# Macaron block on one core: mix norm of rows 6 and 7 traced ahead of the last product's row norms, weight splits ordered behind the last silu or copy

## The chip, the cores and the metric

One core of a Trainium2 chip runs the whole program in one launch. The metric is device microseconds of that core: the median of three runs, and beside it one execution taken by the hardware profiler, to which all rows of the trace belong.

## What is computed

The reference is one layer of an encoder trunk on x of 1024 tokens by 1024 features, all in float32:

```
x = x + 0.5 * RMSNorm_post(SwiGLU_1(RMSNorm_pre(x)))      # d_ff 2816
h = RMSNorm_pre(x); q/k/v = h @ w_qkv
heads = concat(8 grouped-query heads, 8 dilated-window heads)
x = x + RMSNorm_post(heads @ w_out)
x = x + 0.5 * RMSNorm_post(SwiGLU_2(RMSNorm_pre(x)))
SwiGLU(x) = (silu(x @ w_gate) * (x @ w_up)) @ w_down
```

## The kernel before, in words

**Precision.** Every product of matrices is made from a high and a low part of each operand, in three passes (high·high, high·low, low·high). So each loaded weight is split: ScalarE (ACT) copies it to the high part, and GpSimd (POOL) or VectorE (DVE) subtracts that from the weight for the low part. `split` (lines 117 to 119) does this; ACT's half shows as line L118, the other as L119.

**Gate and up.** `Ffn` works through columns i of the hidden width, 1 to 21 (column 0 is done plainly before). A column takes seven products P1 ... P7 instead of eight, from sums of blocks of the operands; `ORDER` gives their order as P1, P6, P2, P7, P5, P4, P3 (the last column has an order of its own). Each product is twelve matmuls at L294 into one of the PSUM banks a, b, c, d. P1 and P2 both accumulate in bank a: after P1, ACT copies the bank to the tile u2 (L416), and only then may P2's matmuls write there, with one product (P6, in bank b) between them. The others are added into u2, u3 and c21 by DVE (L418, L421, L424, L430, L433). `glu` then takes the silu on ACT (L449) and multiplies it with the up half on DVE (L450). In every odd column `keep` writes combinations of the finished hidden tiles to DRAM.

**The weights ahead.** The ring `wgu` has five buffers. `feed` runs before each product and calls `prepare` until five products' weights are made, so ahead of product n the splits of product n + 4 are traced. `prepare` issues the loads of the next column's raw weights on SyncE's queue (SP), the block sums on POOL (L215, L216 before P6, with the sums queued behind P1's low part; L225, L227 after P2, the last of which makes P7's operand), and `split_w`. In trace order a split comes after the silu or copy of the product before, but the framework's scheduler orders each engine's instructions itself: an instruction that it takes to be ready sooner is put first, and the engine then works through its queue in that order. `tc.issue_after(ins)` is the means of holding it: what is traced in its block on the engine of `ins` stands behind `ins` in that queue. It adds no instruction and no semaphore.

**Down and the first tail.** The down product also takes seven products per block, in two groups of inner blocks. `run` goes through all items; a table of jobs gives what is traced after which item, counted from the first item of down product 1 of the second group. For the first FFN the jobs do the work of rows 4 to 7 beside the last two down products: `stat1` (row sums of squares), `post1` (post norm, residual, store of the row tile to `x1d`; L547, L548, L549), `mix1` (the mixing stage's norm: a square with row sum on ACT, L100; a root on ACT, L80; five small operations on DVE; a scale in place on ACT, L647) and `turn1` (eight transposes into PSUM, L107, then high and low part to `actT`, L108 and L109). The last down product, k = 6, finishes rows 0 to 3: for each, `row1` calls `post_late` (half-row square on ACT, L568) and, every second row, `post_scale` (L544, L545) with the store to `x1d`.

**Into the projection.** After `run`, `first(j, T)` is one block of the q/k/v projection: 24 matmuls at L608 for row tile T with weight set j, then an ACT copy (L618), a DVE low part (L619) and two stores. `split_q(1)` splits the second weight set on ACT and DVE (L595, L596). `first(1, 4)` is the first block that needs all of it. The squares of `mix1` write their unused output to slots of `actT`: rows 6, 0, 2 to slot 2, rows 7, 1, 3 to slot 3; `post_late` writes into slot 3 as well:

```
def mix1(Ts):
    r = rms_pair([y[:, T, :] for T in Ts], [junk(T % 2 + 2) for T in Ts])
    for n, T in enumerate(Ts):
        ACT.activation(y[:, T, :], y[:, T, :], AF.Copy, scale=r[n])

def post_late(T):
    ACT.activation(actT[:, HI, 4:8, 3], y[:, T, 512:1024].rearrange("p (k f) -> p k f", k=4), AF.Square,
                   accum_out=SS[T // 2][:, 1, T % 2:T % 2 + 1])
```

So in trace order the square of row 7 came after the four of `post_late`, on one engine.

Of the kernel before, what the change touches and what calls it, by code (L numbers as in the profile page):

```python
# [13 lines left out]
AF = mybir.ActivationFunctionType  # L14
# [22 lines left out]
def tile_macaron_block(ctx, tc, x, f1_pre, f1_post, f1_g, f1_u, f1_d, mix_pre, mix_post, w_qkv,  # L37
                       qg, kg, w_out, f2_pre, f2_post, f2_g, f2_u, f2_d, rope_a, rope_b, mask, out):
    nc = tc.nc
    PE, ACT, DVE, POOL, SP = nc.tensor, nc.scalar, nc.vector, nc.gpsimd, nc.sync  # L40
# [80 lines left out]
    class Ffn:  # L121
# [18 lines left out]
        def __init__(self, wg, wu, wd, tag, far):  # L140
            self.wg, self.wu, self.wd, self.tag, self.far = wg[0], wu[0], wd[0], tag, far
            self.near = "left" if far == "right" else "right"
            self.W, self.RAW, self.H, self.P, self.B, self.Q = {}, {}, {}, {}, {}, {}
            self.A, self.S = {}, {}
            self.items = [("G", i, p) for i in range(1, NF) for p in (self.ORDER if i < NF - 1 else self.LAST)]
            downs = [("D", k, j) for n, g in enumerate(self.GROUPS) for k in self.DOWN[n] for j in g]
            self.items += downs
            self.tiles = []
            for it in self.items:
                self.tiles += [it] if it[0] == "G" else [it + (z,) for z in range(2)]  # L150
            self.wanted = [d[1:] for d in downs]
            self.hd = {}
            for key in self.wanted:
                self.hd[key] = dram.tile([128, 512], F32, name=f"hd{tag}" + "_".join(str(z) for z in key))
            self.made = self.used = 0
            self.dw = {}
            self.late, self.late2 = [], []

        def open_raw(self):
# [48 lines left out]
        def prepare(self, i, prod):  # L208
            a1, b1, a2, b2 = [self.RAW[i, d][:, :, :, 64 * b:64 * b + 64] for d in range(2) for b in range(2)]
            sub, add, tt = OP.subtract, OP.add, POOL.tensor_tensor  # L210
            if i + 1 < NF and prod in ("P1", "P4"):
                self.load_gu(i + 1, ("P1", "P4").index(prod))
            if prod == "P6":
                with tc.issue_after(self.order):
                    tt(b1, b1, b2, op=add)  # L215
                tt(a1, b1, a1, op=sub)  # L216
            if prod == "P7" and i == NF - 1:
                self.S["x"] = self.raw.tile([128, 2, 4, 128], F32, name="rawgu")[:, :, :, 0:64]
                tt(self.S["x"], b2, a1, op=sub)
            src = {"P1": a1, "P6": a1, "P7": self.S.get("x", a1), "P5": b1, "P2": a2, "P4": b2, "P3": a2}[prod]  # L220
            ins = self.split_w((i, prod), src, DVE if (i, prod) == (1, "P6") or prod in ("P5", "P3") else POOL)
            if prod == "P1":
                self.order = ins
            if prod == "P2":
                tt(a2, a2, a1, op=sub)  # L225
                if i < NF - 1:
                    tt(a1, b2, a1, op=sub)  # L227
# [174 lines left out]
        def gate_up(self, i, prod, ps, y, psd):  # L402
            def U(name):
                return self.u.tile([128, 4, 128], F32, name=name, bufs=2 if name == "U2" else 1)

            tt, add, s = DVE.tensor_tensor, OP.add, self.S
            n = (self.ORDER if i < NF - 1 else self.LAST).index(prod)
            if i == 1 and 0 < n < 5:
                self.turn_combo(("T2", "T3", "T1", "T4")[n - 1], y, psd)
            p = self.bank(i, ps, self.BANK[prod])  # L410
            first = prod in ("P1", "P6", "P7", "P5")
            name = {"P1": "B11", "P6": "T2", "P7": "T3", "P5": "T1", "P2": "B21", "P4": "T4", "P3": "B22"}[prod]
            self.product(p, self.W[i, prod], name, first)
            if prod == "P1":
                s["u2"], s["c21"] = U("U2"), U("C21")
                ACT.activation(s["u2"], p, AF.Copy)  # L416
            elif prod == "P6":
                tt(s["u2"], s["u2"], p, op=add)  # L418
            elif prod == "P7":
                s["u3"] = U("U3")  # L420
                tt(s["u3"], s["u2"], p, op=add)  # L421
            elif prod == "P5":
                s["h1"] = self.new_h(i, 1)
                tt(s["u3"], s["u3"], p, op=add)  # L424
                self.glu(s["h1"][64:128], s["u3"], s["c21"])
            elif prod == "P2":
                s["h0"] = self.new_h(i, 0)
                self.glu(s["h0"][0:64], p, s["h0"])
            elif prod == "P4":
                tt(s["c21"], s["u2"], p, op=add)  # L430
                self.glu(s["h0"][64:128], s["c21"], s["h0"])
            elif prod == "P3":
                tt(s["u2"], s["u2"], p, op=add)  # L433
                self.glu(s["h1"][0:64], s["u2"], s["c21"])
            if i == NF - 1 and n == 3:
                self.close_tx(3)
                self.raw.release()
                self.load_left(self.AHEAD)
                self.open_blocks(("b11", "b12"), self.far)
                self.open_blocks(("b22", "b21"), self.near)  # L440
                for j in self.GROUPS[0]:
                    self.load_block(j, "b21")
            if n == 6 and i % 2 == 1:
                self.keep(i // 2)
            if n == 6 and i == NF - 1:
                self.U = [U(name).rearrange("p t f -> p (t f)") for name in ("U2", "U2", "C21", "U3")]

        def glu(self, dst, c, s):
            ACT.activation(s[64:128], c[0:64], AF.Silu)  # L449
            DVE.tensor_tensor(dst, s[64:128], c[64:128], op=OP.mult)  # L450

        def run(self, ps, y, psd, jobs, row):
# [83 lines left out]
    def junk(T):  # L536
        return actT[:, HI, :, T]
# [106 lines left out]
# [4 lines that stand above are left out]
# [9 lines left out]
    def turn1(T):  # L657
        to_actT(T, y[:, T, :], psd)

    def row1(i):  # L660
        post_late(i)
        if i % 2 == 1:
# [5 lines left out]
    f1.run((psg0, psg1), y, psd,  # L668
           {0: [begin1, lambda: stat1((4, 5)), lambda: post1(4)], 1: [lambda: post1(5)], 3: [lambda: mix1((4, 5))],
            5: [early1], 6: [first_q], 7: [lambda: stat1((6, 7)), lambda: post1(6)], 8: [lambda: post1(7)],  # L670
            9: [lambda: turn1(4), lambda: turn1(5)]}, row1)
    psg1.release()
    psg0.release()
    wq1 = open_pool("wq1", side="right")
# [3 lines left out]
    def first(j, T):  # L678
        store_v(j, T, qkv_mm(j, T, psq), wq1)

    mix1((6, 7))
    mix1((0, 1))
    turn1(6)
    first(0, 4)
    turn1(7)
    first(0, 5)
    mix1((2, 3))
    split_q(1, wq1, raw1, "wq1")
    first(0, 6)
# [39 lines left out]
    for nm, g, sc in (("k", kg, None), ("q", qg, 0.125)):  # L729
# [5 lines left out]
        for hf in range(2):  # L735
            for rc in range(2):
                o = 32 * rc + 16 * hf
                s = 32 * rc + 16 * (1 - hf)
# [127 lines left out]
    for j in range(2, 9):  # L866
# [10 lines left out]
        for T in range(NT):  # L877
            p = qkv_mm(j, T, psq)
# [184 lines left out]
    for t in range(NT + 2):  # L1063
        if t < NT:
# [3 lines left out]
            p = pso.tile([128, 1024], F32, name="pz")  # L1068
# [136 lines left out]
```

## Time and profile before

| | us |
|---|---|
| median of 3 runs (lowest, highest) | 2038.99 (2038.28, 2039.86) |
| the profiled execution's own time | 2038.71 |
| its span, first to last instruction | 2036.9 |
| PE (TensorE) busy | 1976.9 |
| ACT busy | 1030.5 |
| DVE busy | 1351.0 |
| POOL busy | 840.7 |

A row of the timeline gives start and length in us, engine, line, operation, output<-inputs by the program's names, shapes and count; in brackets the time that the engine stood idle before it and what ended that. PEld is the load of a matmul's stationary operand, which overlaps the matmul before. A row of the windows gives each engine's busy time in a stretch, then TensorE's granted clock (1.00 is 2.4 GHz, 0.50 is 1.2 GHz) and the share of the DMA engines.

### The profile page before, as it was taken

Reading aid. Unit: us, or ns where it says so; the run is one execution under the profiler, and the core shown is the slowest. Engines: PE = TensorE matmul, PEld = TensorE weight load, DVE = VectorE, ACT = ScalarE, POOL = GpSimd, SP = SyncE. Lnnn points to the kernel's source line nnn. Section 1 sums busy time; section 2 is a strip of 40 time slices with the busy share of each in tenths; the row PEclk is TensorE's granted clock in tenths of the full one; section 3 lists DMA queues with packets and bytes.
Section 4 is the critical chain, followed back from the end, with each engine's and each line's share of the span. In section 5 each row is a group of like instructions: output and inputs, shape, how many; then the busy total and the mean of one; then the engine's idle time right before and its main releaser. Section 6 shows DMA issues by size and latency. Waiting matters only on the chain.

```text
span 2036.9 us, 30471 instructions
## 1 busy us (share of the span) xinstructions
PE 1976.9 (97%) x10704; PEld 1675.1 (82%) x10704; DVE 1351.0 (66%) x2435; ACT 1030.5 (51%) x1977; POOL 840.7 (41%) x768
## 2 busy tenths in 40 slices
PE   7999999999999899999999999999999999999996
PEld 6777777778878699998999998887777777788785
DVE  7645554557878838756989888356545455577787
ACT  5433333334445734547999999234333333344444
POOL 4566656560000002124777887315565666600000
PEclk9999999999999899999999999999999999999998
DMA  5232332428534542232050743322223232375343
GB/s 150 74 102 95 113 103 79 130 82 274 182 109 144 183 131 78 78 93 59 1 140 13 205 133 93 104 78 73 94 88 121 86 104 93 109 268 176 120 130 138
DMA packets 212441, 235.62 MB, mean 116 GB/s; under 512 B 22209, under 2 KB 148161, under 8 KB 212161
## 3 DMA queue, kind: packets, MB, share of 16 engines
q1 hardware_dynamic: 212288, 233.69, 36.7%
q8 instruction: 84, 1.38, 0.3%
q14 instruction: 69, 0.56, 0.1%
HBM read 166.01 MB, written 67.63 MB: 115 GB/s over the span
## 4 chain that ended last, share of the span: by engine, by line
PE 70%; POOL 11%; ACT 6%; DVE 5%; issue 4%; DMA 3%; SPq 0%; DVEq 0%; ACTq 0%; POOLq 0%
PE pq L608 10%; PE pd L368 8%; PE pa L294 8%; PE pc L294 6%; PE pd L294 5%; PE pt L935 5%; POOL wgu L119 5%; PE pz L1073 4%; PE pb L294 3%; PE pa L368 3%; ACT wgu L118 3%; PE po L959 3%; PE pb L368 3%; PE pc L368 3%; PE sp L845 3%
## 5 line engine op out<-in xcount | busy, mean ns | idle before, releaser
L119 POOL TENSOR_TENSOR wgu<-rawgu,wgu 128x512 fp32r<-128x512 f32 x216 | 312.9, 1457 | 359.5 <-ACT wgu L118 333.4
L118 ACT ACTIVATE wgu<-rawgu 128x512 fp32r<-128x512 f32 x302 | 181.7, 628 | 377.6 <-POOL rawgu L227 189.6
L294 PE MATMUL pa<-actT,wgu 128*128 128x512 f32 (+1 forms) x1080 | 268.2, 395 | 7.9 <-ACT U L416 7.9
L294 PEld LDWEIGHTS pa<-actT,wgu 128*128 128x128 f32 x1080 | 197.1, 189 | 63.5 <-ACT U L416 20.1
L368 PE MATMUL pd<-wgu 128*128 128x512 f32 x948 | 236.3, 393 | 7.5 <-DVE wgu L119 6.9
L368 PEld LDWEIGHTS pd<-wgu 128*128 128x128 f32 x948 | 178.3, 189 | 49.2 <-DVE wgu L119 10.6
L608 PE MATMUL pq<-wq,actT 128*128 128x256 f32 x1728 | 217.4, 283 | 0.6 <-DVE actT L109 0.6
L608 PEld LDWEIGHTS pq<-wq,actT 128*128 128x128 f32 x1728 | 208.4, 189 | 1.4 <-DVE actT L109 0.9
L118 ACT ACTIVATE wgu<-b 128x512 fp32r<-128x512 f32 x154 | 97.2, 631 | 218.9 <-PE pd L368 209.6
L73 POOL TENSOR_SCALAR gpost<-gpost 128x1024 f32<-128x1024 f32 x2 | 2.6, 1294 | 387.5 <-DVE wgu L119 194.5
L838 POOL TENSOR_SCALAR P<-P,il 128x1024 f32<-128x1024 f32 (+1 forms) x128 | 130.5, 1020 | 66.7 <-DVE il L837 62.7
L119 DVE TENSOR_TENSOR wgu<-b,wgu 128x512 fp32r<-128x512 f32 x154 | 106.1, 689 | 76.5 <-ACT wgu L118 76.4
L450 DVE TENSOR_TENSOR h<-h,C 64x512 f32<-64x512 f32 x42 | 49.6, 1182 | 160.8 <-ACT h L449 160.8
L939 DVE TENSOR_TENSOR PT<-pt,PT 128x512 fp32r<-128x512 f32 (+1 forms) x256 | 146.0, 611 | 2.0 <-ACT PT L938 2.0
L294 PE MATMUL pc<-actT,wgu 128*128 128x512 f32 x552 | 136.5, 395 | 0.0
L294 PE MATMUL pd<-actT,wgu 128*128 128x512 f32 x552 | 136.0, 395 | 0.0
L938 ACT ACTIVATE PT<-pt 128x512 fp32r<-128x512 f32 (+1 forms) x256 | 125.2, 544 | 12.3 <-PE pt L935 8.8
L935 PE MATMUL pt<-identr,P 128*128 128x128 f32 x896 | 124.9, 274 | 2.0 <-ACT vst L773 1.0
L294 PEld LDWEIGHTS pd<-actT,wgu 128*128 128x128 f32 x552 | 103.4, 187 | 25.3
L294 PEld LDWEIGHTS pc<-actT,wgu 128*128 128x128 f32 x552 | 103.4, 188 | 25.3 <-DVE actT L109 0.4
L294 PE MATMUL pb<-tx,wgu 128*128 128x512 f32 x504 | 122.9, 392 | 0.0
L294 PE MATMUL pc<-tx,wgu 128*128 128x512 f32 x504 | 122.4, 392 | 0.0
(204 smaller groups left out, 3978.6 us busy)
## 6 DMA issues: line engine op xcount, KB each, us to landing
hd<-h SPq DMA_DIRECT2D x154, 256.0 KB, 2.8
h<-hd SPq DMA_DIRECT2D x154, 256.0 KB, 2.9
rawgu<-in_ffn_w_gate_dram SPq DMA_DIRECT2D x88, 256.0 KB, 3.0
rawgu<-in_ffn_w_up_dram SPq DMA_DIRECT2D x88, 256.0 KB, 3.5
b<-in_ffn_w_down_dram SPq DMA_DIRECT2D x88, 256.0 KB, 3.6
bkT<-kd SPq DMA_DIRECT2D x32, 320.0 KB, 7.6
rawq<-in_w_qkv_dram SPq DMA_DIRECT2D x16, 512.0 KB, 4.9
bV<-vd SPq DMA_DIRECT2D x8, 640.0 KB, 3.9
```

The source lines that it names most:

```text
L118: ACT.activation(hi, raw, AF.Copy)
L119: return eng.tensor_tensor(lo, raw, f32(hi), op=OP.subtract).ins
L294: PE.matmul(p[:, c0:c1, :], w[:, a, k, :], self.rhs(name, b, k)[:, c0:c1, :], start=(first and n == 0), stop=(n == 11), skip_group_check=True)
L368: PE.matmul(p, A[:, a, 128 * i:128 * i + 128], B[:, b, :], start=(first and start and j == js[0] and n == 0), stop=(end and j == js[-1] an ...
L608: PE.matmul(p, actT[:, a, k, T, :], WQ[j][:, b, k, :], start=(n == 0), stop=(n == 23))
L838: POOL.tensor_scalar(P[:, 0:w], P[:, 0:w], il, 1.0, op0=OP.mult, op1=OP.mult)
L845: PE.matmul(sp[:, 512 * half:512 * half + 512], col(qT[:, h, :], T), kT[:, a, 512 * half:512 * half + 512], start=(a == 0), stop=(a == 1))
L935: PE.transpose(out=p[:, j, :], in_=col(P, b0 + j), identity=ident)
L938: ACT.activation(hv, p[:, 0:n, :], AF.Copy)
L939: DVE.tensor_tensor(lv, p[:, 0:n, :], f32(hv), op=OP.subtract)
L959: PE.matmul(o, V[:, k, :], pt[:, a, k, :], start=(n == 0), stop=(n == 15))
L1073: PE.matmul(p[:, 512 * dh:512 * dh + 512], actT[:, a, c, T, :], WO[c][:, b, 512 * dh:512 * dh + 512], start=(n == 0), stop=(n == 23))
```

## The change

Two things. First, each ACT instruction that is P1's copy or a silu of `glu` is remembered as `self.mark`, and the ACT half of every gate/up split that `prepare` makes is queued behind the mark that was last set when it is traced. The splits of the down products, and those traced before the first copy, get no such edge. Second, `mix1((6, 7))` moves from behind `run` into the job after item 9, where it stands ahead of `turn1(4)`, `turn1(5)` and of the last down product with its `row1` calls; and `mix1((0, 1))` moves behind `turn1(6)`, `first(0, 4)`, `turn1(7)`, `first(0, 5)`.

```diff
-            self.dw = {}
+            self.dw, self.mark = {}, None
...
-            ins = self.split_w((i, prod), src, DVE if (i, prod) == (1, "P6") or prod in ("P5", "P3") else POOL)
+            with ExitStack() as behind:
+                if self.mark is not None:
+                    behind.enter_context(tc.issue_after(self.mark))
+                ins = self.split_w((i, prod), src, DVE if (i, prod) == (1, "P6") or prod in ("P5", "P3") else POOL)
...
             if prod == "P1":
                 s["u2"], s["c21"] = U("U2"), U("C21")
-                ACT.activation(s["u2"], p, AF.Copy)
+                self.mark = ACT.activation(s["u2"], p, AF.Copy).ins
...
         def glu(self, dst, c, s):
-            ACT.activation(s[64:128], c[0:64], AF.Silu)
+            self.mark = ACT.activation(s[64:128], c[0:64], AF.Silu).ins
...
-            9: [lambda: turn1(4), lambda: turn1(5)]}, row1)
+            9: [lambda: mix1((6, 7)), lambda: turn1(4), lambda: turn1(5)]}, row1)
...
-    mix1((6, 7))
-    mix1((0, 1))
     turn1(6)
     first(0, 4)
     turn1(7)
     first(0, 5)
+    mix1((0, 1))
     mix1((2, 3))
```

## Rows read from the trace of the kernel before

**Rows 1.** The page: busy time of each engine, and the clock in 40 slices.
```profile
PE 1976.9 (97%) x10704; PEld 1675.1 (82%) x10704; DVE 1351.0 (66%) x2435; ACT 1030.5 (51%) x1977; POOL 840.7 (41%) x768
...
PEclk9999999999999899999999999999999999999998
```

**Rows 2.** Waits of PE: who waited for whom, us in total, times, longest.
```profile
PE pa L294 <- ACT U L416: 7.9, 18, 2.2
...
PE pd L107 <- ACT y L647: 4.1, 1, 4.1
```

**Rows 3.** Timeline of PE: starts of P1 in six columns, and one P2.
```profile
77.88 2.96 PE L294 MATMUL pa<-actT,wgu 128*128 128x512 f32 x12
...
97.33 2.96 PE L294 MATMUL pa<-actT,wgu 128*128 128x512 f32 x12
...
142.36 3.07 PE L294 MATMUL pa<-actT,wgu 128*128 128x512 f32 x12 [0.24 <-ACT U L416]
...
452.23 2.96 PE L294 MATMUL pa<-actT,wgu 128*128 128x512 f32 x12
...
1408.70 2.96 PE L294 MATMUL pa<-actT,wgu 128*128 128x512 f32 x12
...
1428.10 2.96 PE L294 MATMUL pa<-actT,wgu 128*128 128x512 f32 x12
...
1782.75 2.96 PE L294 MATMUL pa<-actT,wgu 128*128 128x512 f32 x12
```

**Rows 4.** Timeline of ACT in one column whose P1 starts at 156.35.
```profile
157.20 0.63 ACT L118 ACTIVATE wgu<-rawgu 128x512 fp32r<-128x512 f32 x1 [4.67 <-POOL rawgu L227]
157.86 0.63 ACT L449 ACTIVATE h<-C 64x512 f32<-64x512 f32 x1
...
160.57 0.63 ACT L449 ACTIVATE C<-U 64x512 f32<-64x512 f32 x1 [1.42 <-DVE U L433]
161.23 0.60 ACT L416 ACTIVATE U<-pa 128x512 f32<-128x512 f32 x1
```

**Rows 5.** Timeline of DVE in the same column.
```profile
153.75 0.69 DVE L430 TENSOR_TENSOR C<-U,pc 128x512 f32<-128x512 f32 x1 [0.48 <-PE pc L294]
158.52 1.24 DVE L450 TENSOR_TENSOR h<-h,C 64x512 f32<-64x512 f32 x1 [4.08 <-ACT h L449]
```

**Rows 6.** Timeline of POOL and PE: P7's low part made, P7's matmuls.
```profile
157.91 1.29 POOL L119 TENSOR_TENSOR wgu<-rawgu,wgu 128x512 fp32r<-128x512 f32 x1 [0.74 <-ACT wgu L118]
...
164.78 2.92 PE L294 MATMUL pc<-tx,wgu 128*128 128x512 f32 x12
```

**Rows 7.** Windows behind the last down product: engines' busy time, clock, DMA.
```profile
700.50:704.60 4.10, 0.03 (x1) 0.00 (x0) 3.89 (x20) 4.10 (x10) 0.00 (x0) 0.85 0.85 294
704.60:708.20 3.60, 3.60 (x16) 3.28 (x16) 0.55 (x1) 3.60 (x5) 0.00 (x0) 0.50 0.93 286
708.20:713.00 4.80, 4.21 (x19) 3.91 (x19) 4.80 (x9) 4.80 (x12) 0.00 (x0) 0.50 0.68 258
```

**Rows 8.** Timeline of PE in the same stretch.
```profile
694.71 5.81 PE L608 MATMUL pq<-wq,actT 128*128 128x256 f32 x48
...
717.71 3.08 PE L608 MATMUL pq<-wq,actT 128*128 128x256 f32 x24
...
721.41 3.08 PE L608 MATMUL pq<-wq,actT 128*128 128x256 f32 x24
...
728.82 16.38 PE L608 MATMUL pq<-wq,actT 128*128 128x256 f32 x137
```

**Rows 9.** Timeline of ACT in the same stretch.
```profile
694.27 0.63 ACT L568 ACTIVATE actT<-y 128x512 fp32r<-128x512 f32 x1 [4.86 <-DVE y L386]
...
698.79 1.05 ACT L100 ACTIVATE actT<-y 128x1024 fp32r<-128x1024 f32 x1
...
703.40 4.27 ACT L647 ACTIVATE y<-y,rs_y 128x1024 f32<-128x1024 f32 x4
```

**Rows 10.** Stores of row tiles to x1d: from issue to landing, 8 of them.
```profile
DMA to landing us min/median/max: 2.6/3.0/5.8
```

## The prediction

> **What bounds the kernel now.** I read the page first: PE is busy for 97% of the span and its clock is full in all slices but one inside the span and the last [rows 1]. A change that touches only ACT's queue can therefore pay only where PE stands still or runs at half clock. So the next view is PE's waits, and two of them name work that this change moves [rows 2]: matmuls into bank a that waited for P1's copy (7.9 us, 18 times), and the transposes of row 6, which waited once, 4.1 us, for the scale of `mix1`. The reader is to see that the first is spread over the columns and the second is one hole.
>
> **The columns, where the time is.** Idle time understates the first wait, since a late matmul also spoils the overlap with its weight load; the starts of P1 tell it whole. The shortest column of FFN 1 runs from 77.88 to 97.33, 19.45 us; that of FFN 2 from 1408.70 to 1428.10, 19.40 us. From 77.88 to 452.23 there are 19 columns in 374.35 us, and 19 x 19.45 = 369.55: 4.80 us lost. From 1408.70 to 1782.75 there are 19 in 374.05 us, and 19 x 19.40 = 368.60: 5.45 us lost [rows 3]. Together 10.25 us. Of the 7.9 us of idle in the waits, the two longest stand in column 1 of each FFN (2.2 us, the row's longest, and a shorter one of about the same kind), before any mark exists for the splits concerned, and stay.
>
> **Why it is lost.** ACT's queue in one column shows it [rows 4]. c21 was ready at 153.75 + 0.69 = 154.44 [rows 5], yet P4's silu began at 157.86, because P7's split for the next column stood before it and had waited 4.67 us for POOL's L227. DVE, which also works in order, then stood 4.08 us in L450 for that silu [rows 5]; behind L450 is the addition that P3's silu needs, so that silu came at 160.57 and P1's copy at 161.23. P1's matmuls start at 156.35 and a product takes 19.45 / 7 = 2.8 us, so the bank can be copied from about 159.3: the copy is some 1.9 us late and ends only when PE wants bank a, at about 161.9 (P2 of the column before shows 0.24 us of plain idle [rows 3]).
>
> **Part one, the mark.** It adds no instruction, no DMA and no semaphore. P7's split, traced after P4's silu, must now stand behind it. The silu goes at 154.5, L450 at 155.1, the addition as soon as P3 ends at about 156.4, P3's silu near 157.9 (after P7's split, which still comes when L227 ends), the split of P5 after it, and P1's copy at about 159.3, with nothing in front. It ends 2 us before PE needs the bank. I take the whole 10.25 us. From below the bound is the idle that is seen as such: 7.9 less the two waits in column 1, if the second is put at the row's longest too, 3.5 us. What is late next: the splits, which now stand behind silus. P7's low part ends at 157.91 + 1.29 = 159.20 and its matmuls start at 164.78 [rows 6], 5.6 us of cover; a silu is 0.63 us [rows 4], so a split pushed behind one or two stays covered.
>
> The rule that speaks against this part is the strict first-in, first-out queue that the Trainium skill, "TensorE: Matmul & The Clock Gate", section "Architectural detail: the array is 16× 32×32, not 1× 128×128", gives for ScalarE and VectorE: a queued split now inherits each delay of its silu. The 4.67 us of [rows 4] agrees that a queue is held by its head; by that rule alone each split pays for its silu as each silu paid for the split, and it decides the fourth rival's sign, not this sum.
>
> **Part two, the mix norm.** The hole: PE does two blocks from 694.71 (5.81 us), stands until 704.60 waiting for row 6, and runs at half clock from there to 713.00 [rows 7, 8]. The excess over a full-rate run: from 694.71 to 728.82 are seven blocks and six turns of a row. Later, block plus turn take 721.41 - 717.71 = 3.70 us, a block alone 5.81 / 2 = 2.9. So 6 x 3.70 + 2.9 = 25.1 us against 34.1: 9.0 us, the most that this part can give [rows 8].
>
> Why row 6 is late: row 7's square writes the same slot as `post_late`, and in trace order came last, so it stood behind the four half-row squares that begin at 694.27, and went at 698.79; the root and the scales of both rows wait for it, and the scales came at 703.40 [rows 9]. Traced first, it can go in the 4.86 us that ACT stands idle before 694.27, row 7's tile being done in the main by then. It issues no DMA and no POOL work, so nothing moves on SP or POOL; it passes the transposes of rows 4 and 5 with their copies, the last product with its row norms, and on SP the loads of the second weight set, none of which needs it. Its five small DVE operations lie in the same 4.86 us, which DVE's first evacuation ends; without that cover they would delay the row norms. So the transposes of rows 6 and 7 will be ready within the 5.81 us of the two blocks and PE goes straight on.
>
> What is late next is the second weight set, which `first(1, 4)` needs and which ACT splits between its other work. In the hole ACT is busy without a pause: 4.10 of 4.10, 3.60 of 3.60, 4.80 of 4.80 us [rows 7]. It becomes the bound. What leaves it is a square of 1.05 and two scales of 4.27 / 4 = 1.07: 3.2 us. With ACT no longer short, the weight halves, ready early, also go ahead of the squares of rows 2 and 3, two more of 1.05, so `first(1, 4)` moves from 717.71 to about 712.4, 5.3 us earlier. Bounds: 9.0 us above; below, a loss of 2 us: the scale is in place, so row 7's waits until its store to `x1d` has landed, 2.6 to 5.8 us after issue [rows 10], and it could hold the row norms behind it by some two scales. I take 5.3, nearer to the ACT rows than to the full hole.
>
> The clock fell in this stretch after PE had stood idle, and 7.8 us of PE's busy time ran at 1.2 GHz [rows 7]; at 2.4 GHz that is half, so 3.9 us of the 9.0 is the clock's. The Trainium skill, "TensorE: Matmul & The Clock Gate", section "What's actually happening", says that the gate is opened by recent activity and that its ramp is under 1% of a typical span; by that sentence alone the hole would be worth 9.0 - 3.9 = 5.1 us and the sum 0.2 us less. The row has the price, and I use the row.
>
> **The sum.** 10.25 + 5.3 = 15.55 us off the profiled execution's 2038.71 us (span 2036.9 plus 1.8 around it) is 2023.2 us. The median of the runs is 0.28 above that execution: 2023.4 us. All the edits that are not named cost nothing: the mark is bookkeeping while tracing; moving `mix1((0, 1))` back leaves its squares waiting, as now, for rows 0 and 1.
>
> **The rivals.**
> - The hole moves. PE runs out at about 709 and waits there for the weight set, long enough to fall to half clock again, and part two pays nothing: 2038.99 - 10.25 = 2028.7 us. For it: ACT has no idle time there [rows 7] and its order is the scheduler's. Against it: 3.2 us of its work is gone from the stretch. The half clock that followed the hole in [rows 7] is the price. Chance 0.15.
> - The columns keep their loss. P1's copy stays behind P3's silu, and if the addition before it is still late (DVE's own order is not touched), the copy is late too: only part two, 2038.99 - 5.3 = 2033.7 us. For it: the copy does come right behind that silu [rows 4]. Against it: the 4.08 us of DVE's wait goes. Chance 0.07.
> - The change doesn't do what it says: the scheduler already kept these orders in its own reckoning, or finds new ones as long: 2039 us. Against it: ACT's timeline shows a split in front of a silu that was ready, which the edge forbids [rows 4]. Chance 0.04.
> - Slower: the splits become the bound. P5's split stands behind P3's silu, P2's behind P5's, and POOL's chain behind those. It decides once a split is over 5.6 us later than now [rows 6]; each us beyond costs about one us in each of 38 columns. With 1 us beyond: 38 - 15.55 = 22 us more, 2061 us. For it: the queue is in order and one head holds all. Against it: the silus themselves become earlier. Chance 0.04.
>
> **The numbers.** The forecast has 0.70. A measurement of this kernel can tell about 0.2%, 4.1 us, from no change. The forecast and the first two rivals end below 2034.9, together 0.92; 0.01 of it goes to no change, since the second rival lies only 1.2 us below that bound. So faster has 0.91, no change 0.05, slower 0.04. The range: both parts at their best give 2038.99 - 10.25 - 9.0 = 2019.7, and the lowest of three runs lay 0.7 under the median, so 2018.5 below; the first rival at 2028.7 is inside, and part one at two thirds of its sum with part two at nothing, 2032, is the upper end. That leaves out the other rivals and a rest of the forecast, under 2 in 10.
>
> **What would show it.** Part one is right if all columns 2 to 20 take 19.40 to 19.45 us, the wait of L294 for L416 falls to the two of column 1, and P4's silu stands before P7's split in ACT's timeline; it is wrong if the columns still alternate. Part two is right if row 7's square stands before the half-row squares, L107 no longer waits for L647 and `first(1, 4)` starts 4 to 9 us sooner after the last product; it is wrong if PE idles for the weight set and the clock falls again. A wait of L294 for L119 in the columns would mean the slower rival.

## The result and the profile after

The changed kernel takes 2020.95 us (median of 5 runs, 2019.24 to 2025.49), against 2039.86 us of the kernel before beside it (5 runs, 2038.28 to 2040.48): a ratio of 0.9913, with a 95% interval of 0.9902 to 0.9924. That is 15.5 to 20.0 us less, faster, 2.5 us below the predicted 2023.4 and within the range. Its profiled execution is the fastest of the five, 2019.24 us, with a span of 2017.2. Lines behind the new code have moved by three: L294 is now L297, L416 is L419, L568 is L571, L608 is L611, L647 is L650.

The page of the changed kernel, busy time and clock slices:

```profile
PE 1963.5 (97%) x10704; PEld 1672.0 (83%) x10704; DVE 1364.6 (68%) x2435; ACT 1034.4 (51%) x1977; POOL 835.4 (41%) x768
...
PEclk9999999999999999999999999999999999999998
```

PE does the same 10704 matmuls in 13.4 us less busy time than in [rows 1], since fewer of them run at half clock (the mean clock over the execution is 0.996, against 0.992) and fewer come late on their weight load. The slice at reduced clock in the middle is gone. The waits of PE in the changed kernel (waiter, whom for, us in total, times, longest) answer to [rows 2]:

```profile
PE pa L297 <- ACT U L419: 3.8, 2, 2.2
...
PE pd L107 <- ACT y L650: 1.1, 1, 1.1
...
PE pq L611 <- DVE rs_y L82: 0.6, 1, 0.6
```

Of the 18 waits for P1's copy the two of column 1 are left, and the 4.1 us for row 6's scale have become 1.1 us for row 7's. The timeline of PE in the changed kernel: the starts of P1 between which [rows 3] counted 19 columns, then the stretch of [rows 8].

```profile
77.70 2.96 PE L297 MATMUL pa<-actT,wgu 128*128 128x512 f32 x12
...
447.57 2.96 PE L297 MATMUL pa<-actT,wgu 128*128 128x512 f32 x12
...
687.99 1.03 PE L107 MATMUL pd<-identr,y 128*128 128x128 f32 x8
690.12 0.98 PE L107 MATMUL pd<-identr,y 128*128 128x128 f32 x7 [1.10 <-ACT y L650]
...
703.15 3.08 PE L611 MATMUL pq<-wq,actT 128*128 128x256 f32 x24
...
707.71 3.07 PE L611 MATMUL pq<-wq,actT 128*128 128x256 f32 x24 [0.61 <-DVE rs_y L82]
...
1396.19 2.96 PE L297 MATMUL pa<-actT,wgu 128*128 128x512 f32 x12
...
1764.79 2.96 PE L297 MATMUL pa<-actT,wgu 128*128 128x512 f32 x12
```

FFN 1 takes 447.57 - 77.70 = 369.87 us for 19 columns instead of 374.35, and FFN 2 takes 1764.79 - 1396.19 = 368.60 instead of 374.05: 4.48 + 5.45 = 9.93 us gained, 19.47 and 19.40 us for every column. `first(1, 4)` (703.15) now starts 15.16 us after PE is through with the last product, instead of 23.00 (717.71 - 694.71): 7.8 us sooner.

Cutting both spans at the first matmul of each stage tells where all of it lies (us):

| stage, from its first matmul to the next stage's | before | after | difference |
|---|---|---|---|
| up to the first gate matmul | 14.99 | 14.79 | -0.20 |
| gate and up, FFN 1 | 456.65 | 452.19 | -4.46 |
| down, FFN 1, to its last matmul | 222.85 | 220.78 | -2.07 |
| from there to the eighth projection block | 34.34 | 27.35 | -6.99 |
| rest of the projection | 203.96 | 203.76 | -0.20 |
| attention | 327.57 | 327.24 | -0.33 |
| output projection | 94.62 | 95.94 | +1.32 |
| gate and up, FFN 2 | 447.15 | 442.11 | -5.04 |
| down, FFN 2 | 221.85 | 220.13 | -1.72 |
| end | 12.93 | 12.92 | -0.01 |

Two parts of the sum are the change's: 9.5 us in the gate stages and 7.0 us behind the last down product. The two down stages, with 3.8 us, have no edit in their matmuls; of what they show the section on the hardware tells more.

The 7.0 us hold against this one execution of the kernel before. Six experiments below also leave the mix norm at its place in the trace, and their profiles give 34.1, 34.3 and 34.0 us for the same stage (experiments 1, 5, 8) and 32.5, 32.4 and 32.6 (experiments 4, 6, 7). The windows of the stage, of the kernel before and of experiment 6, show what differs (busy time of PE, PEld, DVE, ACT, POOL, then clock and DMA):

```profile
694.49:728.83 34.34, 29.67 (x219) 28.80 (x217) 23.04 (x63) 26.02 (x55) 0.00 (x0) 0.85 0.59 189
```

```profile
689.81:722.24 32.43, 27.76 (x218) 26.89 (x217) 22.96 (x63) 25.88 (x55) 0.00 (x0) 0.89 0.63 203
```

At a clock of 0.85 some (1 - 0.85) x 2 x 34.34 = 10.3 us of it ran at 1.2 GHz, at 0.89 some 7.1 us. With the move the stage takes 27.1 to 27.4 us in every profile of experiments 2, 3, 9, 10 and 11 too, so its gain is 5.1 to 7.2 us, by how long the half clock lasted without it.

**The column, on ACT and DVE.** Timelines of the changed kernel, the column whose P1 starts at 155.57, ACT first and then DVE:

```profile
153.75 0.63 ACT L452 ACTIVATE h<-C 64x512 f32<-64x512 f32 x1 [1.52 <-DVE C L433]
156.78 0.63 ACT L118 ACTIVATE wgu<-rawgu 128x512 fp32r<-128x512 f32 x1 [2.39 <-POOL rawgu L230]
157.44 0.63 ACT L452 ACTIVATE C<-U 64x512 f32<-64x512 f32 x1
158.09 0.63 ACT L118 ACTIVATE wgu<-rawgu 128x512 fp32r<-128x512 f32 x1
158.63 0.58 ACT L419 ACTIVATE U<-pa 128x512 f32<-128x512 f32 x1
```

```profile
154.41 1.17 DVE L453 TENSOR_TENSOR h<-h,C 64x512 f32<-64x512 f32 x1 [0.76 <-ACT h L452]
155.77 0.69 DVE L436 TENSOR_TENSOR U<-U,pd 128x512 f32<-128x512 f32 x1 [0.18 <-PE pd L297]
```

P4's silu stands first and does not wait for POOL; DVE's product with the up half, which waited 4.08 us for it in [rows 5], waits 0.76; P1's copy starts 158.63 - 155.57 = 3.06 us after its P1, in place of 161.23 - 156.35 = 4.88 in [rows 4].

**The transition, on ACT.** Windows of the changed kernel behind the last down product (busy time of PE, PEld, DVE, ACT, POOL, then clock and DMA), then ACT's timeline there:

```profile
687.80:700.00 12.20, 11.10 (x94) 10.78 (x93) 12.02 (x36) 11.93 (x31) 0.00 (x0) 1.00 0.65 223
700.00:715.00 15.00, 14.39 (x125) 14.18 (x124) 10.41 (x22) 10.91 (x20) 0.00 (x0) 1.00 0.74 227
```

```profile
682.68 1.06 ACT L100 ACTIVATE actT<-y 128x1024 fp32r<-128x1024 f32 x1
...
683.86 0.29 ACT L80 ACTIVATE rs_t<-ss,eps 128x2 f32<-128x2 f32 x1
686.15 1.15 ACT L650 ACTIVATE y<-y,rs_y 128x1024 f32<-128x1024 f32 x1 [2.00 <-DVE rs_y L88]
687.55 0.63 ACT L571 ACTIVATE actT<-y 128x512 fp32r<-128x512 f32 x1 [0.24 <-DVE y L389]
...
688.93 1.13 ACT L650 ACTIVATE y<-y,rs_y 128x1024 f32<-128x1024 f32 x1
...
697.88 1.72 ACT L598 ACTIVATE wq<-rawq,gm 128x256 fp32r<-128x256 f32 x4
...
703.67 1.06 ACT L100 ACTIVATE actT<-y 128x1024 fp32r<-128x1024 f32 x1 [1.64 <-DVE y L548]
```

Row 7's square (682.68), the root and row 6's scale all stand ahead of the first half-row square (687.55), which was the head of the stretch in [rows 9]. Row 7's scale comes at 688.93, behind two half-row squares and half a microsecond after its store to `x1d` has landed (688.42 by the trace). ACT's weight halves end at 697.88 + 1.72 = 699.60, 3.5 us before `first(1, 4)` starts, and two scales later ACT even stands idle for 1.64 us. The clock is 1.00 in both windows, against 0.50 in [rows 7]. Two rows of DVE and two of ACT tell what came next:

```profile
703.55 0.48 DVE L599 SCALAR_TENSOR_TENSOR wq<-rawq,gm,wq 128x256 fp32r<-128x256 f32 x1
...
707.14 0.42 DVE L622 TENSOR_TENSOR vst<-pq,vst 128x256 fp32r<-128x256 f32 x1
```

```profile
705.68 1.06 ACT L100 ACTIVATE actT<-y 128x1024 fp32r<-128x1024 f32 x1
...
706.72 0.38 ACT L621 ACTIVATE vst<-pq 128x256 fp32r<-128x256 f32 x1
```

The last low part of the weight set (703.55) is made while `first(1, 4)` already runs; PE doesn't stop for it. The 0.61 us before the block at 707.71 are named after the norm's reciprocal (L82), but by the program a block reads `actT` and the weights alone. It writes one of three PSUM banks, and its bank, that of the third block, is emptied by DVE's L622 at 707.14 + 0.42 = 707.56. L622 needs ACT's copy (L621), which stands in ACT's queue behind the squares of rows 2 and 3 (703.67 and 705.68).

### The profile page after: what moved, and what is told of

Read it like the earlier page. It is cut to its first block, busy times and chain, and to the rows that moved or that the text cites. A ratio compares the mean times of both kernels' runs of the same rounds, so it can differ in the third digit from the quotient of the medians.

```text
span 2017.2 us, 30479 instructions
## 1 busy us (share of the span) xinstructions
PE 1963.5 (97%) x10704; PEld 1672.0 (83%) x10704; DVE 1364.6 (68%) x2435; ACT 1034.4 (51%) x1977; POOL 835.4 (41%) x768
## 4 chain that ended last, share of the span: by engine, by line
PE 88%; DVE 4%; ACT 3%; issue 2%; DMA 2%; POOL 1%; SPq 0%; ACTq 0%; POOLq 0%; DVEq 0%
PE pc L297 12%; PE pa L297 12%; PE pd L297 11%; PE pq L611 9%; PE pd L371 9%; PE pb L297 6%; PE pt L937 5%; PE pa L371 3%; PE pb L371 3%; PE pc L371 3%; PE po L961 3%; PE sp L847 3%; PE pz L1075 3%; PE po L972 2%; PE sp L919 2%
## 5 line engine op out<-in xcount | busy, mean ns | idle before, releaser
L119 POOL TENSOR_TENSOR wgu<-rawgu,wgu 128x512 fp32r<-128x512 f32 x216 | 295.1, 1368 | 356.8 <-ACT wgu L118 332.7
L118 ACT ACTIVATE wgu<-rawgu 128x512 fp32r<-128x512 f32 x302 | 189.9, 631 | 341.1 <-POOL rawgu L216 156.8
L297 PE MATMUL pa<-actT,wgu 128*128 128x512 f32 (+1 forms) x1080 | 264.9, 392 | 3.8 <-ACT U L419 3.8
L297 PEld LDWEIGHTS pa<-actT,wgu 128*128 128x128 f32 x1080 | 199.7, 189 | 50.9 <-ACT U L419 4.3
L611 PE MATMUL pq<-wq,actT 128*128 128x256 f32 x1728 | 214.6, 281 | 0.6 <-DVE rs_y L82 0.6
L611 PEld LDWEIGHTS pq<-wq,actT 128*128 128x128 f32 x1728 | 206.1, 188 | 0.9 <-PE pd L107 0.8
L453 DVE TENSOR_TENSOR h<-C,U 64x512 f32<-64x512 f32 x84 | 87.7, 1044 | 95.3 <-ACT C L452 95.1
L297 PE MATMUL pc<-actT,wgu 128*128 128x512 f32 x552 | 136.5, 395 | 0.0
L297 PE MATMUL pd<-actT,wgu 128*128 128x512 f32 x552 | 136.1, 394 | 0.0
L297 PEld LDWEIGHTS pd<-actT,wgu 128*128 128x128 f32 x552 | 103.4, 187 | 25.3
L297 PEld LDWEIGHTS pc<-actT,wgu 128*128 128x128 f32 x552 | 103.4, 188 | 25.4 <-DVE actT L109 0.4
L297 PE MATMUL pb<-tx,wgu 128*128 128x512 f32 x504 | 122.9, 392 | 0.0
L297 PE MATMUL pc<-tx,wgu 128*128 128x512 f32 x504 | 122.4, 391 | 0.0
```

The lines of the kernel that those rows point to most:

```text
L118: ACT.activation(hi, raw, AF.Copy)
L119: return eng.tensor_tensor(lo, raw, f32(hi), op=OP.subtract).ins
L297: PE.matmul(p[:, c0:c1, :], w[:, a, k, :], self.rhs(name, b, k)[:, c0:c1, :], start=(first and n == 0), stop=(n == 11), skip_group_check=True)
L611: PE.matmul(p, actT[:, a, k, T, :], WQ[j][:, b, k, :], start=(n == 0), stop=(n == 23))
```

## The experiments

The kernels ran in three batches of four, each on one chip with its own runs of the kernel before: 2038.78 us (median of 28 runs), 2038.86 (7) and 2040.43 (11). Ratios are against these. Stages and columns are read from each kernel's profiled execution.

**1. The marks alone.** The changed kernel with the job, and the order behind `run`, as before:

```diff
-            9: [lambda: mix1((6, 7)), lambda: turn1(4), lambda: turn1(5)]}, row1)
+            9: [lambda: turn1(4), lambda: turn1(5)]}, row1)
...
+    mix1((6, 7))
+    mix1((0, 1))
     turn1(6)
...
-    mix1((0, 1))
     mix1((2, 3))
```

> The marks alone, the mix norm where it was. Theory: the two parts are independent, the marks are worth the columns' loss, 10 us: about 2029.5, every column of 2 to 20 at 19.40 to 19.47 us, and the hole of 4 us before row 6's transposes with its half clock still there. Rival (the parts need each other, the columns' share is smaller than read): 2033 or more.

2026.24 us (7 runs), ratio 0.9952 (0.9938 to 0.9966), 6.9 to 12.6 us less. Columns of 19.47 and 19.40 us, as in the changed kernel; from the last down matmul to the eighth block 34.07 us, as before. The marks have all of the gain in the columns and nothing of that in the transition.

**2 and 3. The moves alone.** The kernel before with both calls of `mix1` moved (2), and with `mix1((6, 7))` alone moved, `mix1((0, 1))` staying ahead of `turn1(6)` (3):

```diff
-            9: [lambda: turn1(4), lambda: turn1(5)]}, row1)
+            9: [lambda: mix1((6, 7)), lambda: turn1(4), lambda: turn1(5)]}, row1)
...
-    mix1((6, 7))
```

> The two moves of the mix norm alone, no marks. Theory: the stretch behind the last down product shortens by 7 us as it did in the changed kernel, so about 2032.5; the columns keep their alternation of 19.5 and 19.9 us. Rival (the stretch gained only because the columns before it put the engines into another order): nothing, 2039.

> Only the mix norm of rows 6 and 7 moves; that of rows 0 and 1 stays ahead of the transposes of row 6; no marks. Theory: the first move has all of the gain, within 1 us of the run with both moves, 2032 to 2033.5. Rival: with rows 0 and 1 still traced first, their squares and scales stand before the weight halves on ScalarE and 2 to 4 us of the gain are lost, 2034.5 to 2036.5.

2035.00 us, ratio 0.9981 (0.9970 to 0.9993), and 2033.18 us, 0.9977 (0.9967 to 0.9987), 10 runs each. The transition takes 27.14 and 27.29 us, so the first move has all of the gain and the second is worth nothing that can be measured. The columns still alternate between 19.5 and 20.0 us. The medians are 3.8 and 5.6 us down where the transition's profile has 5.1 to 7.2 us less; in both profiled executions the down stage of FFN 1 was 1.2 to 1.4 us longer than in that of the kernel before, with a second stretch at half clock (last section).

**4. The slot alone.** The kernel before, with squares of rows 6 and 7 written to slots that `post_late` does not use, in the old trace order:

```diff
-        r = rms_pair([y[:, T, :] for T in Ts], [junk(T % 2 + 2) for T in Ts])
+        r = rms_pair([y[:, T, :] for T in Ts], [junk(T % 2 + (0 if T > 5 else 2)) for T in Ts])
```

> The kernel before, in its old trace order, with one thing changed: the unused output of the squares of rows 6 and 7 goes to slots 0 and 1 and not to 2 and 3, where the half-row squares write. Theory (row 7's square was late because it shares a slot with the row norms and so had to follow them): the square goes before the half-row squares and most of the hole closes, 2032 to 2035. Rival (it was late because it was traced later, and ready work that is traced first wins): the hole stays, 2039.

2040.66 us (10 runs), ratio 1.0009 (0.9998 to 1.0019): nothing gained. ACT's timeline of this kernel:

```profile
689.89 1.06 ACT L100 ACTIVATE actT<-y 128x1024 fp32r<-128x1024 f32 x1
...
696.33 0.63 ACT L568 ACTIVATE actT<-y 128x512 fp32r<-128x512 f32 x1 [5.29 <-DVE y L386]
...
700.65 0.47 ACT L80 ACTIVATE rs_t<-ss,eps 128x2 f32<-128x2 f32 x2
...
705.61 4.25 ACT L647 ACTIVATE y<-y,rs_y 128x1024 f32<-128x1024 f32 x4
```

The slot did hold row 7's square: it goes at 689.89 now, ahead of the half-row squares. But the root still comes at 700.65, behind all four of them, though both squares were done by 691.04 and ACT then stood idle for 5.29 us. The scales come no earlier against the row norms, and PE waits 4.2 us as before. (The stage takes 32.5 us in this profile, 1.9 less than in that of the kernel before; experiments 6 and 7 show the same with the slot shared.) So the trace order keeps the root and the scales back, beyond any wait for a slot, and the slot explains the square alone.

**5 and 6. One edge, and all but that one.** The marks alone (experiment 1), with the edge only on P7's split (5), and on all but P7's (6):

```diff
-                if self.mark is not None:
+                if self.mark is not None and prod == "P7":
```

> Of all the edges only one per column is kept: P7's split behind the silu of the product traced before it, P4's. No move of the mix norm. Theory (that one split, waiting for GpSimd's block sum in front of a silu that was ready, is the whole cause): as with all marks, about 2029.5 and columns of 19.40 to 19.47 us. Rival (P5's split in front of P3's silu counts as well): some columns stay over 19.5 us and the time is 2031 to 2035.

> The opposite: all marks but the edge of P7's split, no move of the mix norm. Theory: P4's silu stays behind P7's split and the columns keep their loss, within 2 us of 2039. Rival: the other edges bring half or more, 2034 or less.

2027.41 us, ratio 0.9943 (0.9928 to 0.9958), and 2029.32 us, 0.9949 (0.9934 to 0.9964), 4 runs each. Both have columns of 19.47 and 19.40 us only. The single edge on P7's split is enough; but the other edges, without it, do as well, which the theory excluded. ACT's timeline of experiment 6 shows how:

```profile
233.44 0.63 ACT L452 ACTIVATE h<-C 64x512 f32<-64x512 f32 x1 [1.53 <-DVE C L433]
236.44 0.63 ACT L118 ACTIVATE wgu<-rawgu 128x512 fp32r<-128x512 f32 x1 [2.36 <-POOL rawgu L230]
```

Nothing orders P7's split behind P4's silu here, and still it stands there: the scheduler put it there. A new theory: the edge on P2's split makes POOL's chain behind it late in the scheduler's reckoning, so that P7's operand, and with it P7's split, seems ready later than the silu. The next pair tests it.

**7 and 8. P5's edge alone, and P2's edge alone.** As experiment 5, with `"P5"` and with `"P2"` in the condition:

> One edge per column, another one: only P5's split behind P3's silu, no move of the mix norm. In the kernel's order on ScalarE P7's split still stands before P4's silu, P5's split now stands between P3's silu and P1's copy. Theory (the columns lose because P1's copy stands behind a chain that P7's split starts): the chain is as late as before and P1's copy 0.65 us later, so each of 38 columns is 0.4 to 0.65 us longer than before, 15 to 25 us slower, about 2059. Rival (any split put behind its silu helps): as with all marks, 2026 to 2029.

> One edge per column, a third: only P2's split behind P5's silu, no move of the mix norm. With it the scheduler by itself puts P7's split behind P4's silu, though no edge asks for that. Theory (what counts is which of these two stands first): full gain of the marks, columns of 19.40 to 19.47 us, 2026 to 2029. Rival (the edge of P7's split or of P5's is needed): columns as before, 2037 to 2040.

P5's edge alone: 2058.84 us, ratio 1.0092 (1.0074 to 1.0109), 15.1 to 22.2 us slower than the kernel before, as its theory had it. P2's alone: 2027.66 us, 0.9940 (0.9924 to 0.9955), the full gain (4 runs each). ACT's timeline with P5's edge alone, PE's timeline and its waits, and ACT's wait for POOL's L227, which is now L230:

```profile
219.56 0.63 ACT L118 ACTIVATE wgu<-rawgu 128x512 fp32r<-128x512 f32 x1 [4.66 <-POOL rawgu L230]
220.22 0.63 ACT L452 ACTIVATE h<-C 64x512 f32<-64x512 f32 x1
222.92 0.63 ACT L452 ACTIVATE C<-U 64x512 f32<-64x512 f32 x1 [2.08 <-DVE U L436]
223.58 0.63 ACT L118 ACTIVATE wgu<-rawgu 128x512 fp32r<-128x512 f32 x1
224.11 0.58 ACT L419 ACTIVATE U<-pa 128x512 f32<-128x512 f32 x1
```

```profile
224.75 3.07 PE L297 MATMUL pa<-actT,wgu 128*128 128x512 f32 x12 [0.84 <-ACT U L419]
```

```profile
PE pa L297 <- ACT U L419: 23.9, 38, 2.2
...
ACT wgu L118 <- POOL rawgu L230: 189.6, 40, 7.2
```

Of the kernel before, the row that [rows 4] leaves out between the two silus, and the same wait:

```profile
158.51 0.63 ACT L118 ACTIVATE wgu<-rawgu 128x512 fp32r<-128x512 f32 x1
```

```profile
ACT wgu L118 <- POOL rawgu L227: 189.6, 40, 7.2
```

P7's split stands in front of P4's silu here as it did in the kernel before, and in both of them in every column: 40 waits for POOL, 189.6 us. So the columns of 19.5 us there had the late silu too; in the one of [rows 4] the copy of P1 ended at 161.23 + 0.60 = 161.83, just before P2's matmuls wanted the bank at 161.91 by PE's timeline. What P5's edge moves is P5's split. It stood between the two silus (158.51) and now stands between P3's silu and P1's copy (223.58), and the copy starts 0.53 us behind the start of that split. That half microsecond makes 38 waits for P1's copy of the 18 in [rows 2], columns of 20.0 and 20.5 us by turns where they took 19.5 and 19.95, and gate stages of 466.43 and 458.72 us, 9.8 and 11.6 more than before. With P2's edge alone, ACT's timeline has the silu first:

```profile
232.26 0.63 ACT L452 ACTIVATE h<-C 64x512 f32<-64x512 f32 x1 [1.53 <-DVE C L433]
235.24 1.15 ACT L118 ACTIVATE wgu<-rawgu 128x512 fp32r<-128x512 f32 x2 [2.35 <-POOL rawgu L230]
```

With five products ahead, every kernel here that has P4's silu in front of P7's split has 19.40 and 19.47 us alone in columns 2 to 20, and every one that has it behind has longer ones; what else stands before P1's copy adds to them. An edge can also turn an order that it does not name, as P2's does. That it does so by way of POOL's chain in the scheduler's reckoning is not shown, and no run shows why every second column is the longer one.

**9 and 10. Less weight ahead.** The changed kernel with splits of gate and up made four (9) or three (10) products ahead instead of five, save in the last columns. This puts every split one or two products later, where the slower rival says they become the bound:

```diff
-            while self.made < len(self.tiles) and self.made - self.used < self.WBUFS:
+            lim = 4 if self.items[0][0] == "G" and self.used < 7 * (NF - 1) - 5 else self.WBUFS
+            while self.made < len(self.tiles) and self.made - self.used < lim:
```

> The changed kernel with the weights of a gate/up product made four products ahead and not five, so that each split stands behind a mark one product (2.8 us) later. Theory (5.6 us of cover under the splits): 2.8 us are left, no column waits for a split, time as the changed kernel within 2 us, 2019 to 2023. Rival (the splits are near to being the bound): waits of matmuls for L119 in the columns, 10 us or more slower.

> The same with three products ahead, two products (5.6 us) later than in the changed kernel, all of the cover that the prediction read. Theory: the splits of P6 and P7, which also wait for four block sums on GpSimd, come at or behind their matmuls; 0.3 to 1 us per column lost, 10 to 40 us slower than the changed kernel, with waits for L119. Rival (the cover is larger than read, since a split is ready long before its mark is asked): no change.

Four ahead: 2025.14 us, ratio 0.9929 (0.9914 to 0.9944), columns of 19.47 and 19.40 us: one product, 2.8 us, later costs the columns nothing. Three ahead: 2077.09 us, 1.0187 (1.0170 to 1.0204), 4 runs each. PE's waits and one place of its timeline with three ahead:

```profile
PE pc L298 <- POOL wgu L119: 22.3, 38, 0.6
```

```profile
231.71 2.58 PE L298 MATMUL pc<-tx,wgu 128*128 128x512 f32 x10 [0.55 <-POOL wgu L119]
```

P7 waits for its low part in all 38 columns, which take 20.3 and 21.0 us by turns; the two gate stages are 22.7 and 21.8 us longer than the changed kernel's, some 1.1 us a column. With the splits two products (5.6 us) later, and if each us beyond the cover costs a column one us, as the prediction had it, the cover is about 5.6 - 1.1 = 4.5 us. That is an estimate: with one run beyond the cover, its size and the price of a us cannot be told apart.

**11 and 12. The changed kernel again, and what it leaves.** Two waits stay in the changed kernel: in column 1, where no mark exists yet, and for row 7's scale. Experiment 12 makes fewer splits before the first two products and hangs the first ones behind the last copy of the operands' transposes; and it holds row 7's transposes behind the first projection block:

```diff
+            lim = {0: 3, 1: 2}.get(self.used, self.WBUFS)
-            while self.made < len(self.tiles) and self.made - self.used < self.WBUFS:
+            while self.made < len(self.tiles) and self.made - self.used < lim:
...
+            self.mark = MARK["turn"]
...
     first(0, 4)
-    turn1(7)
+    with tc.issue_after(MARK["mm"]):
+        turn1(7)
```

(`MARK["turn"]` is the last ACT copy of the transposes in `turn_combo`, `MARK["mm"]` the last matmul of the block before.)

> The changed kernel once more, beside the next run on the same chip. Theory: 2019 to 2025, columns of 19.40 and 19.47 us, 27.3 us from the last down product to the eighth block of the projection.

> The changed kernel with two more orders. In column 1 the splits of P7 and the later products are made only after P1's copy and the turned T2 are queued, so that P1's copy no longer stands behind P7's split there either; and the transposes of row 7 stand behind the first block of the projection, not before it. Theory (the same cause in column 1: 2.2 and 1.6 us of waits for P1's copy, and 1.1 us for row 7's scale): 3 to 5 us faster than the changed kernel beside it. Rival (column 1 is bound by the turning of the combined rows, and the idle time only moves): within 1 us of it.

The changed kernel: 2023.94 us (6 runs), ratio 0.9919 (0.9904 to 0.9933). Experiment 12: 2018.32 us (2015.71 to 2021.24, 4 runs), ratio 0.9893 (0.9878 to 0.9908), 5.6 us under it on the same chip and the lowest median here. The wait for P1's copy is gone from PE's waits, the one for row 7's scale is 0.2 us, and the gate stages take 450.38 and 439.63 us, against 454.16 and 443.69 in experiment 11 and 452.19 and 442.11 in the first profile of the changed kernel. The gate stages' gain is thus 7.8 us against the one execution of the changed kernel and 4.3 us against the other, and the two intervals of ratios overlap from 0.9904 to 0.9908. Against it, the down stage of FFN 1 took 226.13 us in this profile, 4.9 us more than in experiment 11, with two stretches at half clock. That experiment 12 is faster is likely, how much is open.

## Why the prediction was right

**The total** was 15.55 us against 15.5 to 20.0 measured at first, so at the lower edge, and 13.7 to 19.6 in experiment 11. The two parts add up within the scatter: 12.5 us (experiment 1) and 3.8 us (experiment 2) of median are 16.3, against 16.5 in experiment 11 (2040.43 - 2023.94); by the ratios they are 9.8 and 3.9 us, with intervals that together reach from 8.3 to 18.7.

**Part one** came as worked out: 9.93 us of 10.25, every column at the length of the shortest one, two waits left in column 1, the silu in front of the split. Counting lost time by the starts of P1, and not by the 7.9 us of idle in [rows 2], was what gave the size. The chain that the forecast gave (split, silu, DVE in order, the next silu, copy) is shown at both ends: take the split from in front of the silu and every column is short (experiment 5), put half a microsecond more before P1's copy and PE waits for it 38 times instead of 18 (experiment 7). Not foreseen was that P7's own edge is not needed (experiments 6 and 8). The prediction held the edges to be a matter of what each one forbids; they can also change orders that they do not name. Experiment 7 shows the price of one order that it did name, "the split of P5 after it": that split lands between P3's silu and P1's copy. In the changed kernel it is harmless there, since P3's silu comes early (157.44, and the copy at 158.63); without P7's edge it costs half a microsecond a column.

**Part two** took 5.3 us; the stage gave 7.0 in the first pair of profiles (34.34 to 27.35), and 5.1 to 7.2 by which kernel without the move stands beside it. The hole and what closes it were right, what would bound the stage next was not. The step that failed is "It becomes the bound", said of ACT and the second weight set. PE never waited for that set: ACT's halves were done at 699.60, 3.5 us early, because without the hole they also passed the squares of rows 2 and 3, as the prediction had it, and because row 6's root, scale and row 7's square had left the stretch altogether (row 7's scale, which the sum had leaving as well, stayed). What was late next was row 7's scale (1.10 us of idle), which the lower bound named for its store, and ACT's copy of the third block, which stood behind the squares of rows 2 and 3 (0.61 us): 1.7 of the 2.0 us by which the 7.0 stay under the 9.0 of the full hole. The cause, too, was only half right. "Row 7's square shares the slot" holds for the square alone; experiment 4 shows that the trace order also keeps the root and scales behind, and the prediction would have expected most of the gain from the slot alone.

The half clock went with the hole: 0.50 in [rows 7], 1.00 after. Its price shows in the kernels that keep the hole: with some 10.3 us at half clock the stage took 34.0 to 34.3 us, with some 7.1 it took 32.4 to 32.6, so about 3 us of half clock cost about 1.7 us, half of them, as [rows 7] priced it. The sentence of the Trainium skill, "TensorE: Matmul & The Clock Gate", section "What's actually happening", that a ramp is under 1% of a typical span, is no price for one hole: 3.9 us are under 1% of this span as well. The 5.1 us that the prediction set beside its own value by that sentence are therefore no second forecast, though three of the profiles come near them.

**The rivals.** *The hole moves* did not happen: no stretch at half clock is left between 687.80 and 715.00. *The columns keep their loss* and *doesn't do what it says* are excluded by the columns. *The splits become the bound* did not happen either, and experiments 9 and 10 show where it lies: nothing is lost at 2.8 us of delay and 1.1 us a column at 5.6, so the cover is under the 5.6 us read from [rows 6], some 4.5 if each us beyond it costs one. The strict order of ScalarE's queue, which the same page of the Trainium skill gives in "Architectural detail: the array is 16× 32×32, not 1× 128×128", agrees with the 4.66 us of experiment 7, where a ready silu stood behind a waiting split.

**Not foreseen** was 1.3 us more in the output projection (its transposes wait 1.1 us for DVE), where the change has no line, and the 3.8 us less in the down stages. With the small differences of the other stages they are the 3.2 us by which the 19.7 us of the span pass the 9.5 and 7.0 of the two parts.

## What to carry to other kernels

Look at an in-order engine's queue for the instruction that stood ready behind a waiting head, and follow it to what PE wanted: a split that could wait some microseconds cost 10 us in two stages because a silu stood behind it. Where a scheduler orders the queues, read the order after each edit. An edge can change an order that it does not name (on P2's split: 0.6% faster), and it can put its own instruction in a worse place (P5's split, in front of the copy that PE waits for: 0.9% slower). When work seems held by a shared buffer, give it another buffer alone as a test: here the square moved and nothing else did.

## What the runs showed of the hardware

The clock's fall is not the same behind each wait of the same length. In the down stage of FFN 1, PE waits 2.92 us for the same low part in the kernel before, in the changed kernel and in experiment 3, and some 22 us later 2.1 us for another. Windows that begin with the first wait, of the kernel before, of the changed kernel and of experiment 3, which has also one around the second wait (columns as above):

```profile
662.00:670.00 8.00, 5.08 (x15) 3.89 (x15) 7.31 (x17) 7.24 (x16) 0.00 (x0) 0.79 0.74 242
```

```profile
657.00:665.00 8.00, 5.08 (x23) 4.11 (x23) 8.00 (x19) 7.77 (x17) 0.00 (x0) 1.00 0.75 242
```

```profile
661.00:669.00 8.00, 5.08 (x16) 3.71 (x15) 7.74 (x17) 7.67 (x16) 0.00 (x0) 0.79 0.73 226
686.00:694.00 8.00, 5.87 (x20) 4.39 (x19) 6.17 (x13) 4.85 (x8) 0.00 (x0) 0.79 0.71 228
```

PE is busy for the same 5.08 us in the first three, but does 15 matmuls at a clock of 0.79 and 23 at 1.00: after the wait part of the stretch ran at 1.2 GHz in one and all of it at 2.4 GHz in the other. In experiment 3 the shorter wait was followed by a fall as well, which it was not in the kernel before. The share that runs at half clock, (1 - 0.79) x 2 x 8 = 3.4 us, costs half of itself, 1.7 us. One or two of these more or less can make up much of the 6 us between the fastest and the slowest run of the changed kernel, whose mean clocks are 0.996 and 0.993. They are also most of the 2.07 us that the down stage of FFN 1 shows in the table, and as much of the 1.72 us of FFN 2's, where the profile has 6.8 us at half clock before and 3.4 after.

FFN 1's part may yet be the marks'. In the four profiles without them (the kernel before, experiments 2, 3 and 4) the stage has one or two stretches at half clock and takes 222.9 to 224.2 us; in the seven with marks, or one edge of them, and five products ahead (the changed kernel, experiments 1, 5, 6, 7, 8 and 11) it has none and takes 220.4 to 221.4. The marks with less made ahead (experiments 9, 10 and 12) have such stretches again, with 224.0 to 226.1 us. PE's wait of 2.92 us stands in all of them. What in the marks would keep the clock up no run shows.
